# The second block's mixer projections in plain float32: one product on raw weights in place of three float32r products on split ones

## The chip, the cores and the metric

The kernel runs on one core of one Trainium2 chip. Such a core has TensorE (PE in the profile; its weight loads are listed apart as PEld), VectorE (DVE), ScalarE (ACT), GpSimd (POOL) and SyncE (SP), which here only issues DMA transfers. Each engine works through its own instructions in order, and semaphores order the engines among each other. The metric is the device time of one execution, in microseconds (us), lower being better.

## The reference

A residual stream of 256 tokens with 1024 channels goes through two models one after the other, each with two layers. The change touches the second model only, and in it one part of each layer, the mixer:

```python
hn = _modulate(_rms_norm(h, norm_g[l, 1]), sh2, sc2)
z = hn @ w_in[l]                       # 1024 -> 2564 columns
o_a = _differential_attention(qa, ka, va, ...)   # slices of z, normalised per head
o_b = _conformer_conv(z[..., CONV0:GMLP0], ...)  # gate, causal convolution of width 31, norm, swish
o_c = _chunked_spatial_gating(z[..., GMLP0:FOX_Q0], ...)
o_d = _forgetting_attention(qd, kd, vd, log_f)
mixed = jnp.concatenate([o_a, o_b, o_c, o_d], axis=-1)
h = h + g2[:, None, :] * (mixed @ w_out[l])      # 1024 -> 1024
```

Before and after the mixer stands a gated feed-forward part (`ffn1`, `ffn2`) with its own norm and modulation. All is float32.

## The kernel before

Activations lie feature-major: 128 channels on the partitions, 256 tokens in the free dimension, so that 1024 channels are eight "k tiles" of 256 columns. Every large product is built from steps of one k tile by 128 output columns, which accumulate in a PSUM bank.

**Three float32r products for one float32 product.** The kernel multiplies in the type float32r and splits both operands into a high and a low part to keep float32 accuracy. For a weight part of 128 x 1024 numbers, `split_to` (L223) has ACT cast the raw weights `raw` to `wh`, and then DVE or POOL subtract to get `wl`; `prog["pool"]` says that every so-many-th subtraction goes to POOL (1: all of them, 3: every third). Activations are split by `hilo` (L202: a cast on ACT, a subtraction on DVE). `mm3` (L284) then issues three matmuls into the same bank: high by high, low activation by high weight, high activation by low weight. An `Act` holds an activation's two parts; a `Shifted` holds the unnormalised activation with two more columns for the shift, so that the first chunk of a projection can run before the norm is known.

**The weight stream.** All large weights lie in one array in the order of use and are loaded in parts of up to 512 KB (`load_to`, L214), each by one DMA of the SP queue, into five buffers `raw`. A load is issued five parts ahead, a part is split three ahead, and the two halves have four buffers each. A load into a buffer waits until the last reader of its former content is done; the SP queue issues in order, so that what stands behind such a load waits with it.

**The order of the work.** The program is recorded in the order of the Python code. The projections go chunk by chunk (`chunk`, L268), and at each weight part `fill()` (L241) lets the background generators take a step: the norms of queries and keys, the convolution, the attentions, the spatial gate. Thus the products are interleaved on PE with the small matmuls of the attentions, and on DVE the 62 steps of the convolution with the norms.

**The mixer** (L1124 to L1382, twice). It loads two small tables `v2` and `ws` (in the profile `v` and `ws`) by the SP queue, and starts with instructions on them (`lp`, `ls`). Then: the first chunk M of 512 columns with the unnormalised activation (bank `m`); beside it the norm (`nrm`, `nu`, `rs`) and the normalised activation `h` (`xn`, `hh`, `hl`). The bank `m` goes through Tanh into the convolution `cv`. Four chunks of 256 columns give queries and keys (`qk`), each followed by its norm: square, matmul `qn`, a reciprocal root in three steps on DVE (`qu`, `qu`, `qr`), and the multiplication into `qk` or `fqk`. The scores `ds` of the first attention stand on PE right behind the fourth chunk. Chunks `gv` (260 columns), `gu` (256) and `mv` (512, weights as moving operand) follow, with the scores `ds`, `fs`, the convolution's norm `cc` and the transposes `tr` between them. The output projection N (`mo`) takes up the four branches (`mix`) two k tiles at a time. Per layer that is 21 weight parts of M and 8 of N. In the last quarter of the feed-forward part ahead of the mixer, `ffn` sets `prog["pool"] = 1` (L1108), which holds until the last part of N.

The names in the rows: `fd` is the bank of the feed-forward part's second product, `x` the residual stream, `xh`/`xl` its `Shifted` form, `f` the bank of the feed-forward part's first product, `sq` and `ssum` the sums of squares for the norm, `lfr` the forget gates of the second attention.

Of the kernel before, what the change touches and what calls it, by code (L numbers as in the profile page):

```python
# [24 lines left out]
RETH = 8  # L25
SUB_COLS = 1024
POOL_EVERY = 3
MLA_SCALE = (64 + 32) ** -0.5
# [94 lines left out]
def tile_model(ctx: ExitStack, tc: tile.TileContext, xT: bass.AP, pos: bass.AP, cvec: bass.AP, wst: bass.AP,  # L123
# [81 lines left out]

# [1 line left out]
    subs = _subs()  # L207
# [33 lines left out]
    def fill():  # L241
        """One step of each background part that is due."""
        prog["fill"] += 1
        for g in list(bgs):
            if prog["fill"] >= due[g]:
                step(g)

    def step(g):
        """A part yields the number of fills until its next step."""
        try:  # L250
            due[g] = prog["fill"] + next(g)
        except StopIteration:
            bgs.remove(g)
# [14 lines left out]
    def chunk(key, l, k0, kk, c0, cc):  # L268
# [6 lines left out]
        while s < len(subs) and subs[s][0] == j:  # L275
            split_to(s + 3)
            _, k, n, _, _ = subs[s]
            wh, wl = split.pop(s)
            for i in range(n):
                yield k0 + k + i, wh[:, i * cc:(i + 1) * cc], wl[:, i * cc:(i + 1) * cc]  # L280
            fill()
            s += 1
# [19 lines left out]
    def gemm_last(c, a, banks, klast, done):  # L302
        """The last part of a product, bank by bank, each followed by what takes it up."""
        parts = list(chunk(*c))
        for j in range(c[5] // 256):
            for k, wh, wl in parts:
                for e in range(2):
                    m = 2 * j + e
                    mm3(banks[j], banks[j].t[:, e * 256:e * 256 + 256], wh[:, m * P:(m + 1) * P],
                        wl[:, m * P:(m + 1) * P], a.h(k), a.l(k), k == klast)  # L310
# [11 lines left out]
    def gemm_shift(c, xa, banks, after):  # L322
        """The product with an unnormalised activation; the shift's products follow in two more columns."""
        for k, wh, wl in chunk(*c):
            if k == 2:
                after()
            for m, b in enumerate(banks):
# [3 lines left out]
                b.mm(b.t[:, :258], wb, xa.h(k), stop=k == 7)  # L331

    def pair_outs(banks):
        return {m: (banks[m // 2], m % 2) for m in range(2 * len(banks))}

# [1 line left out]
    nc.scalar.preload_act_table_set("silu_and_others")  # L337
# [43 lines left out]
    class Act:  # L381
        """A feature-major activation of n tiles as high and low float32r parts."""

# [7 lines left out]
        def l(self, k, n=1):  # L391
            return self.lo[k // 4][:, (k % 4) * 256:(k % 4 + n) * 256]

    gfa = const([P, 8], "gfa")
# [112 lines left out]

# [1 line left out]
    cond = []  # L509
# [503 lines left out]

    # =================== block 2 ===================
    rsx = rs_t
# [3 lines left out]
    def normalised(dst, l, i, first=False):  # L1019
        """rmsnorm(x) * g * (1 + scale) + shift in two parts, and the factor of the unnormalised product."""  # L1020
        if first:
# [10 lines left out]
        for j in range(4):  # L1032
            t_ = t2("xn")
            mul(v3(t_, 2), v3(xk(2 * j, 2), 2), bc(r, 2))
            for e in range(2):
                k = 2 * j + e
                nc.vector.tensor_scalar(out=t_[:, e * 256:(e + 1) * 256], in0=t_[:, e * 256:(e + 1) * 256],  # L1037
                                        scalar1=acol[:, k:k + 1],
                                        scalar2=mods[l][:, 24 * i + k:24 * i + k + 1], op0=ALU.mult, op1=ALU.add)
            hilo(t_, dst.h(2 * j, 2), dst.l(2 * j, 2))  # L1040
        if first:
# [9 lines left out]
    def following(l, i):  # L1051
        l, i = (l, i + 1) if i < 2 else (l + 1, 0)
        if l == L:
            return None
        return Shifted(l, i, lambda k: scl[l][:, 8 * i + k:8 * i + k + 1])

# [10 lines left out]

    def shift_bias(bank):
        b = small("bias", 1)
        nc.vector.tensor_reduce(out=b, in_=bank.t[:, 256:258], axis=AX.X, op=ALU.add)  # L1070
        return b

    def ffn(l, f, i, xa, first=False):
# [50 lines left out]
    def mixer(l, xa):  # L1124
# [29 lines left out]
        mix = Act(8, "mix")  # L1154

# [18 lines left out]
        def conv():  # L1174
# [26 lines left out]
            mul(v3(cv, 2), v3(bn_.t, 2), bc(r_, 2))  # L1201
            o_ = t2("co")
            for i in range(2):
                ins = act(o_[:, i * 256:(i + 1) * 256], cv[:, i * 256:(i + 1) * 256], AF.Silu,
                          scale=vc(f"cng{l}", i), bias=vc(f"cnb{l}", i))
            base_table(ins)
            hilo(o_, mix.h(4, 2), mix.l(4, 2))

        for i in range(2):
            ba, bg_ = b4[2 * i], b4[2 * i + 1]  # L1210
            ca, cg = shift_bias(ba), shift_bias(bg_)
            nc.vector.tensor_scalar_mul(cg, cg, 0.5)
# [10 lines left out]
        def diff(i):  # L1223
# [38 lines left out]
            rsqrt_eps(b.t[:, 0:256], r_, u_)  # L1262
            stt(r_, o_, dog, r_, ALU.mult, ALU.mult)
            hilo(r_, mix.h(6 + i), mix.l(6 + i))

        def fox(i):
# [32 lines left out]
            pv(b_o, lambda e, kb: vt[:, kb * 512 + 256 + (2 * i + e) * 64:kb * 512 + 320 + (2 * i + e) * 64], pts)  # L1299
            hilo(b_o.t[:, 0:256], mix.h(2 + i), mix.l(2 + i))  # L1300

# [3 lines left out]
        for n, (name, dst, blk, g) in enumerate((("qa", qk, "blk32", gq_), ("ka", qk, "blk32", vc(f"dqk{l}", 1)),  # L1305
                                                 ("fq", fqk_, "blk64", gf_), ("fk", fqk_, "blk64", vc(f"fqk{l}", 1)))):
            b = Bank("qk", True)
            gemm([("M", l, 0, 8, 512 + 256 * n, 256)], h.h, h.l, pair_outs([b]), 7)
# [3 lines left out]
        gemm_tok([("M", l, 0, 8, 1536, 260)], h.h, h.l, [(b, 0) for b in bg], 7)  # L1312
        vn = u4("vn", 512)
# [15 lines left out]
        def spatial():  # L1329
# [24 lines left out]
            mul(so, so, ut)  # L1354
            hilo(so, mix.h(0, 2), mix.l(0, 2))

        bu = Bank("gu", True)
        gemm([("M", l, 0, 8, 1796, 256)], h.h, h.l, pair_outs([bu]), 7)
        ins = act(ut, bu.t, AF.Gelu_apprx_tanh)
# [4 lines left out]
        bv = [Bank("mv", True) for _ in range(2)]  # L1364
        gemm_tok([("M", l, 4 * i, 4, 2052, 512) for i in range(2)], h.h, h.l, [(b, 0) for b in bv], 7)
        for t in range(2):
# [168 lines left out]
```

## Time and profile before

| | |
|---|---|
| Median of three runs | 2057.26 us (2048.43 to 2058.85) |
| Profiled execution: span from first to last instruction | 2054.9 us; what lies around the span is not shown, the median of the runs is 2.4 us longer |
| First mixer, from the first `m` product to the last `mo` product | 1162.06 to 1309.25 us: 147.2 us |
| Second mixer | 1706.69 to 1854.10 us: 147.4 us |
| PE busy / weight loads busy | 96% / 92% of the span |
| DVE, ACT, POOL busy | 72%, 51%, 35% |
| HBM traffic | 402.96 MB read, 197 GB/s over the span |

A matmul's busy time in the profile is from its start to its modelled end; matmuls overlap, so the pace of a stream is read from start to start in the timeline and not from the busy time of one. A float32 matmul of the program is recorded as two matmuls, one behind the other. The granted clock of PE (PEclk) is shown as a share of 2.4 GHz: 1.00 is that level, 0.50 is the other level of 1.2 GHz, and what lies between is a mean over a stretch.

### The profile page before, as it was taken

Reading aid. Unit: us, or ns where it says so; the run is one execution under the profiler, and the core shown is the slowest. Engines: PE = TensorE matmul, PEld = TensorE weight load, DVE = VectorE, ACT = ScalarE, POOL = GpSimd, SP = SyncE. Lnnn points to the kernel's source line nnn. Section 1 sums busy time; section 2 is a strip of 40 time slices with the busy share of each in tenths; the row PEclk is TensorE's granted clock in tenths of the full one; section 3 lists DMA queues with packets and bytes.
Section 4 is the critical chain, followed back from the end, with each engine's and each line's share of the span. In section 5 each row is a group of like instructions: output and inputs, shape, how many; then the busy total and the mean of one; then the engine's idle time right before and its main releaser. Section 6 shows DMA issues by size and latency. Waiting matters only on the chain. (4 is left out here: it accounts for less than half of the span.)

```text
span 2054.9 us, 38413 instructions
## 1 busy us (share of the span) xinstructions
PE 1966.4 (96%) x15570; PEld 1894.0 (92%) x15570; DVE 1480.6 (72%) x2076; ACT 1045.8 (51%) x1584; POOL 717.9 (35%) x339
## 2 busy tenths in 40 slices
PE   8999999999999999999999978998999998789999
PEld 7989999999989999999999966898999998679999
DVE  6778778696667778699877598888574446968443
ACT  5656555445556545345444446644454444455442
POOL 3232242323331343334223653422332246443222
PEclk9999999999999999999999989999999999899999
DMA  7545556885445656886667522388546554324553
GB/s 248 169 165 207 209 175 244 306 317 206 144 144 190 227 188 227 309 295 216 242 260 252 183 93 93 124 289 302 183 151 215 179 178 134 108 93 165 184 175 125
DMA packets 114946, 406.52 MB, mean 198 GB/s; under 512 B 12880, under 2 KB 14672, under 8 KB 114768
## 3 DMA queue, kind: packets, MB, share of 16 engines
q1 hardware_dynamic: 114768, 404.06, 56.6%
q8 instruction: 122, 2.00, 0.4%
q14 instruction: 56, 0.46, 0.1%
HBM read 402.96 MB, written 1.05 MB: 197 GB/s over the span
## 5 line engine op out<-in xcount | busy, mean ns | idle before, releaser
L233 POOL TENSOR_TENSOR wl<-raw,wh 128x1024 fp32r<-128x1024 f32 (+2 forms) x253 | 635.0, 2514 | 1257.7 <-ACT wh L231 1182.8
L231 ACT CAST wh<-raw 128x1024 fp32r<-128x1024 f32 (+1 forms) x627 | 641.4, 1030 | 614.7 <-PE fd L172 113.4
L233 DVE TENSOR_TENSOR wl<-raw,wh 128x1024 fp32r<-128x1024 f32 (+1 forms) x374 | 497.3, 1335 | 248.6 <-ACT wh L231 246.1
L172 PE MATMUL f<-hh,wl 128*128 128x256 f32 x1280 | 363.9, 285 | 4.9 <-POOL wl L233 4.0
L172 PE MATMUL f<-hl,wh 128*128 128x256 f32 x1280 | 364.2, 285 | 3.2 <-DVE hl L194 2.9
L172 PE MATMUL f<-hh,wh 128*128 128x256 f32 x1280 | 363.1, 284 | 4.3 <-ACT hh L203 3.1
L185 DVE SCALAR_TENSOR_TENSOR ada<-ada,cond 128x1024 f32<-128x1024 f32 x144 | 227.8, 1585 | 94.9 <-DMA ada<-ada_dram 94.6
L172 PEld LDWEIGHTS f<-hh,wl 128*128 128x128 f32 x1280 | 246.8, 193 | 6.4 <-POOL wl L233 4.6
L172 PEld LDWEIGHTS f<-hl,wh 128*128 128x128 f32 x1280 | 246.9, 193 | 4.8 <-DVE hl L194 4.8
L172 PEld LDWEIGHTS f<-hh,wh 128*128 128x128 f32 x1280 | 246.6, 193 | 5.1 <-ACT hh L203 3.7
L172 PE MATMUL fd<-hidh,wl 128*128 128x256 f32 x704 | 200.4, 285 | 4.0 <-DVE wl L233 3.5
L172 PE MATMUL fd<-hidh,wh 128*128 128x256 f32 x704 | 200.0, 284 | 0.6 <-DVE x L185 0.6
L172 PE MATMUL fd<-hidl,wh 128*128 128x256 f32 x704 | 199.9, 284 | 0.0
L172 PE MATMUL pr<-hh,wh 128*128 128x256 f32 x672 | 194.8, 290 | 0.0
L172 PE MATMUL pr<-hh,wl 128*128 128x256 f32 x672 | 190.1, 283 | 0.0
L172 PE MATMUL pr<-hl,wh 128*128 128x256 f32 x672 | 190.0, 283 | 0.0
L172 PE MATMUL dn<-hidh,wl 128*128 128x256 f32 x512 | 146.2, 285 | 3.6 <-DVE wl L233 3.6
L172 PE MATMUL u<-hh,wl 128*128 128x256 f32 x512 | 145.9, 285 | 2.6 <-DVE wl L233 2.6
L172 PE MATMUL u<-hh,wh 128*128 128x256 f32 x512 | 145.9, 285 | 0.0
L172 PE MATMUL dn<-hidh,wh 128*128 128x256 f32 x512 | 145.6, 284 | 0.0
L172 PE MATMUL dn<-hidl,wh 128*128 128x256 f32 x512 | 145.5, 284 | 0.0
L172 PE MATMUL u<-hl,wh 128*128 128x256 f32 x512 | 145.5, 284 | 0.0
(474 smaller groups left out, 4786.1 us busy)
## 6 DMA issues: line engine op xcount, KB each, us to landing
raw<-wst_dram SPq DMA_DIRECT2D x599, 512.0 KB, 4.0
ada<-ada_dram SPq DMA_DIRECT2D x144, 512.0 KB, 5.0
raw<-wst_dram SPq DMA_DIRECT2D x22, 256.0 KB, 2.8
raw<-wst_dram SPq DMA_DIRECT2D x4, 390.0 KB, 3.0
R<-ret_dram SPq DMA_DIRECT2D x2, 512.0 KB, 7.7
out_dram<-x SPq DMA_DIRECT2D x8, 128.0 KB, 3.3
C<-cst_dram SPq DMA_DIRECT2D x1, 896.0 KB, 7.7
v<-vec_dram SPq DMA_DIRECT2D x2, 448.0 KB, 5.7
```

The costliest lines, as they stand in the source:

```text
L172: nc.tensor.matmul(out, lhsT=lhsT, rhs=rhs, start=grp not in self.open, stop=stop, skip_group_check=True)
L185: nc.vector.scalar_tensor_tensor(out=out, in0=in0, scalar=s, in1=in1, op0=op0, op1=op1, **kw)
L231: nc.scalar.copy(wh[:, :n * cc], src)
L233: ins = eng.tensor_tensor(out=wl[:, :n * cc], in0=src, in1=wh[:, :n * cc].bitcast(F32), op=ALU.subtract)
```

## The change

The chunks of M and N are no longer split. `split_to` hands the raw part on as it was loaded, and the products take raw float32 weights and one float32 activation: a class `Plain` (one tile set in place of two) for `h` and `mix`, a class `ShiftedPlain` for the mixer's unnormalised activation with one more column in place of two. Each `mm3` of three float32r matmuls becomes one float32 matmul. With the halves go the casts and subtractions of these weights (29 parts per layer) and the second halves of `xa`, `h` and `mix`; the four results that fed a `hilo` are written straight into `mix`. The line that set `prog["pool"] = 1` ahead of the mixer goes, so the last weight parts of that feed-forward part are shared between DVE and POOL as the earlier ones are. (Removed comment lines are left out here.)

```diff
+NATIVE = ("M", "N")
...
-            _, _, n, cc, _ = subs[i]
+            j, _, n, cc, _ = subs[i]
+            if plan[j][0] in NATIVE:
+                split[i] = (raws.pop(i), None)
+                prog["split"] += 1
+                continue
...
+    def gemm_native(chunks, a, outs, klast):
+        for c in chunks:
+            for k, w, _ in chunk(*c):
+                for m in range(c[5] // P):
+                    bank, half = outs[m]
+                    bank.mm(bank.t[:, half * 256:half * 256 + 256], w[:, m * P:(m + 1) * P], a.f(k), stop=k == klast)
+    def gemm_tok_native(chunks, a, outs, klast):
...
+                    bank.mm(bank.t[:, c0:c0 + c[5]], a.f(k)[:, t * P:(t + 1) * P], w, stop=k == klast)
+    def gemm_shift_native(c, xa, banks, after):
...
+                b.mm(b.t[:, :257], w[:, m * P:(m + 1) * P], xa.f(k), stop=k == 7)
...
-            hilo(t_, dst.h(2 * j, 2), dst.l(2 * j, 2))
+            if not plain:
+                hilo(t_, dst.h(2 * j, 2), dst.l(2 * j, 2))
...
-            if m == 3:
-                prog["pool"] = 1 if i == 0 else 2
+            if m == 3 and i == 2:
+                prog["pool"] = 2
...
-        h, r = Act(8, "h"), rsx
+        h, r = Plain(8, "h"), rsx
...
-        gemm_shift(("M", l, 0, 8, 0, 512), xa, b4, lambda: next(normalised(h, l, 1)))
+        gemm_shift_native(("M", l, 0, 8, 0, 512), xa, b4, lambda: next(normalised(h, l, 1)))
...
-            stt(r_, o_, dog, r_, ALU.mult, ALU.mult)
-            hilo(r_, mix.h(6 + i), mix.l(6 + i))
+            stt(mix.f(6 + i), o_, dog, r_, ALU.mult, ALU.mult)
...
-                gemm([("N", l, 2 * i, 2, 0, 1024)], mix.h, mix.l, pair_outs(b4), 7)
+                gemm_native([("N", l, 2 * i, 2, 0, 1024)], mix, pair_outs(b4), 7)
```

**PE, between the second and third chunk of queries and keys in the first layer's mixer.** The rows before (`hh`, `hl` are the activation's halves, `wh`, `wl` the weight's):

```order
L172 MATMUL qk_13780<-hh_13580,wh_13713 128x256
L172 MATMUL qk_13780<-hl_13582,wh_13713 128x256
L172 MATMUL qk_13780<-hh_13580,wl_13714 128x256
L172 MATMUL qk_13851<-hh_13579,wh_13783 128x256
L172 MATMUL qk_13851<-hl_13581,wh_13783 128x256
L172 MATMUL qk_13851<-hh_13579,wl_13784 128x256
```

And the rows now, from the first chunk's end to the third chunk:

```order
L173 MATMUL qk_13667<-h_13559,raw_13511 128x256 x8
L173 MATMUL qk_13698<-h_13558,raw_13564 128x256 x8
L173 MATMUL qn_13713<-qsq_13696,C 128x512
L173 MATMUL qk_13698<-h_13559,raw_13574 128x256 x8
L173 MATMUL qk_13739<-h_13558,raw_13610 128x256 x8
L173 MATMUL qn_13754<-qsq_13737,C 128x512
```

Three matmuls of a product became one that reads the loaded buffer itself; the small matmuls stand at the same places between the chunks, here and in the rest of the mixer.

**POOL, from the last quarter of the first layer's first feed-forward part on.** Before, behind the third sum of squares (`ssum` x2), the subtractions of all the following weights, those of M and N among them:

```order
L374 TENSOR_TENSOR ssum<-ssum,sq_13367 128x256 x2
L233 TENSOR_TENSOR wl_13439<-raw_13317,wh_13438 128x1024
L233 TENSOR_TENSOR wl_13469<-raw_13347,wh_13468 128x512
L233 TENSOR_TENSOR wl_13499<-raw_13376,wh_13498 128x1024
L233 TENSOR_TENSOR wl_13529<-raw_13406,wh_13528 128x1024
```

Now, from the same sum to the end of the mixer and the next feed-forward part:

```order
L405 TENSOR_TENSOR ssum<-ssum,sq_13358 128x256 x2
L238 TENSOR_TENSOR wl_14413<-raw_14337,wh_14412 128x1024
L402 TENSOR_TENSOR ssum<-sq_14389 128x256
L405 TENSOR_TENSOR ssum<-ssum,sq_14402 128x256 x2
L405 TENSOR_TENSOR ssum<-ssum,sq_14422 128x256 x2
L238 TENSOR_TENSOR wl_14559<-raw_14377,wh_14558 128x1024
```

POOL has nothing to do during the mixer; its next subtraction belongs to the feed-forward part behind it.

**DVE, at the end of the first layer's first feed-forward part.** Before (`x<-fd` is the update of the residual stream, `lp` the first instruction on the table `v`):

```order
L185 SCALAR_TENSOR_TENSOR x<-fd_13196,hg_164,x 128x256 x2
L185 SCALAR_TENSOR_TENSOR xl_12813<-x,scl_162,xh_12810 128x256 x2
L1130 MEMSET yv_13554 128x576
L188 TENSOR_TENSOR lp_13562<-v_2050_13552 128x32 x2
L1138 TENSOR_REDUCE ls_13563<-lp_13562 128x1 x2
L185 SCALAR_TENSOR_TENSOR x<-fd_13375,hg_164,x 128x256 x2
L188 TENSOR_TENSOR ws_13553<-ws_13553,C 128x128 x3
```

Now:

```order
L238 TENSOR_TENSOR wl_13428<-raw_13308,wh_13427 128x1024
L238 TENSOR_TENSOR wl_13458<-raw_13338,wh_13457 128x512
L186 SCALAR_TENSOR_TENSOR x<-fd_13364,hg_164,x 128x256 x2
L1193 MEMSET yv_13533 128x576
L189 TENSOR_TENSOR lp_13541<-v_2044_13531 128x32 x2
L1201 TENSOR_REDUCE ls_13542<-lp_13541 128x1 x2
L189 TENSOR_TENSOR ws_13532<-ws_13532,C 128x128 x4
```

The last update of the stream stood behind the two instructions on the table and now stands ahead of them; among the last weight subtractions ahead of it two are now on DVE.

## Rows read from the trace of the kernel before

**Rows 1.** The page's head and part 1: engine, busy us (share), instructions.

```profile
span 2054.9 us, 38413 instructions
PE 1966.4 (96%) x15570; PEld 1894.0 (92%) x15570; DVE 1480.6 (72%) x2076; ACT 1045.8 (51%) x1584; POOL 717.9 (35%) x339
```

**Rows 2.** Stretches of both mixers: length, busy us (instructions) by engine, PEclk, DMA.

```profile
1162.06:1309.25 147.19, 122.05 (x833) 108.23 (x831) 126.44 (x246) 77.70 (x156) 73.82 (x30) 0.90 0.32 109
1706.69:1854.10 147.41, 120.82 (x833) 106.62 (x832) 125.08 (x245) 77.70 (x156) 74.06 (x30) 0.90 0.32 108
```

**Rows 3.** Waits of PE in the first mixer: us in total, times, longest.

```profile
PE ds L172 <- DVE qk L185: 8.9, 1, 8.9
PE cc L172 <- DVE cv L185: 4.7, 1, 4.7
PE fs L172 <- DVE lfr L1273: 3.5, 1, 3.5
PE nrm L172 <- ACT sq L378: 2.9, 1, 2.9
PE qk L172 <- ACT hh L203: 2.3, 2, 1.9
```

**Rows 4.** Stretches of 5 us around the wait of `ds`, columns as in Rows 2.

```profile
1215.00:1220.00 5.00, 0.00 (x0) 0.00 (x0) 5.00 (x10) 0.01 (x1) 0.77 (x1) 0.74 0.46 156
1220.00:1225.00 5.00, 4.00 (x21) 3.35 (x22) 5.00 (x12) 0.58 (x1) 0.00 (x0) 0.50 0.00 0
```

**Rows 5.** Timeline of PE, float32r products: start us, length us, instruction.

```profile
1199.25 0.28 PE L172 MATMUL qk<-hl,wh 128*128 128x256 f32 x1
...
1199.61 0.28 PE L172 MATMUL qk<-hl,wh 128*128 128x256 f32 x1
...
1242.70 0.39 PE L172 MATMUL mv<-wl,hh 128*128 128x512 f32 x1
...
1243.39 0.39 PE L172 MATMUL mv<-wl,hh 128*128 128x512 f32 x1
```

**Rows 6.** Timeline of PE, float32 products of 256 and 512 columns.

```profile
91.35 0.60 PE L172 MATMUL sc<-KE,Q 128*128 128x256 f32 x2
91.79 0.59 PE L172 MATMUL sc<-KO,Q 128*128 128x256 f32 x2
92.22 0.22 PE L172 MATMUL sc<-mkb,identb 128*128 128x128 bf16 x1
...
1194.69 1.02 PE L172 MATMUL qn<-qsq,C 128*128 128x512 f32 x2
...
1195.66 0.28 PE L172 MATMUL qk<-hl,wh 128*128 128x256 f32 x1
```

**Rows 7.** DVE in the first mixer, one group of lines: count, busy us, mean ns.

```profile
L185 DVE SCALAR_TENSOR_TENSOR cv<-yv,cw,cv 128x256 f32<-128x256 f32 x60 | 36.9, 660 | 0.0
```

**Rows 8.** Timeline of POOL and DVE in the first mixer.

```profile
1191.79 20.71 POOL L233 TENSOR_TENSOR wl<-raw,wh 128x1024 fp32r<-128x1024 f32 x7 [5.46 <-ACT wh L231]
...
1199.07 2.90 DVE L185 SCALAR_TENSOR_TENSOR qu<-qu,qr 128x512 f32<-128x512 f32 x1
...
1224.70 0.68 DVE L185 SCALAR_TENSOR_TENSOR qu<-qu,qr 128x512 f32<-128x512 f32 x1
1225.30 0.47 DVE L185 SCALAR_TENSOR_TENSOR cv<-yv,cw,cv 128x256 f32<-128x256 f32 x1
1225.70 0.68 DVE L185 SCALAR_TENSOR_TENSOR qr<-qu,qr 128x512 f32<-128x512 f32 x1
```

**Rows 9.** Timeline of SP and DVE at the start of the first mixer.

```profile
1159.02 0.42 SPq L1127 DMA_DIRECT2D v<-vec_dram  x1
...
1164.43 2.28 DVE L188 TENSOR_TENSOR lp<-v 128x32 f32<-128x32 f32 x2 [12.60 <-DMA v<-vec_dram]
...
1166.86 0.87 DVE L185 SCALAR_TENSOR_TENSOR x<-fd,hg,x 128x256 f32<-128x256 f32 x2
```

More of the change, by code (lines that the diff above doesn't have):

```diff
@@ L279, in chunk @@
             for i in range(n):
-                yield k0 + k + i, wh[:, i * cc:(i + 1) * cc], wl[:, i * cc:(i + 1) * cc]
+                yield k0 + k + i, wh[:, i * cc:(i + 1) * cc], wl[:, i * cc:(i + 1) * cc] if wl is not None else None
             fill()
@@ L308, in gemm_last @@
                     m = 2 * j + e
-                    mm3(banks[j], banks[j].t[:, e * 256:e * 256 + 256], wh[:, m * P:(m + 1) * P],
-                        wl[:, m * P:(m + 1) * P], a.h(k), a.l(k), k == klast)
-            done(j)
+                    out, cols = banks[j].t[:, e * 256:e * 256 + 256], slice(m * P, (m + 1) * P)
+                    if wl is None:
+                        banks[j].mm(out, wh[:, cols], a.f(k), stop=k == klast)
+                    else:
+                        mm3(banks[j], out, wh[:, cols], wl[:, cols], a.h(k), a.l(k), k == klast)
+            done(j)
+    def gemm_native(chunks, a, outs, klast):
[5 more added lines that the diff above has]
+    def gemm_tok_native(chunks, a, outs, klast):
+        for c in chunks:
+            for k, w, _ in chunk(*c):
+                for t in range(2):
+                    bank, c0 = outs[t]
+                    bank.mm(bank.t[:, c0:c0 + c[5]], a.f(k)[:, t * P:(t + 1) * P], w, stop=k == klast)
     def gemm_tok(chunks, ah, al, outs, klast):
@@ L331, in gemm_shift @@
                 b.mm(b.t[:, :258], wb, xa.h(k), stop=k == 7)
+    def gemm_shift_native(c, xa, banks, after):
+        for k, w, _ in chunk(*c):
+            if k == 2:
+                after()
+            for m, b in enumerate(banks):
+                b.mm(b.t[:, :257], w[:, m * P:(m + 1) * P], xa.f(k), stop=k == 7)
     def pair_outs(banks):
@@ L392, in l, with __init__, f, parts @@
             return self.lo[k // 4][:, (k % 4) * 256:(k % 4 + n) * 256]
+    class Plain:
+        def __init__(self, n, s):
+            self.t = [u4(s) for _ in range((n + 3) // 4)]
+        def f(self, k, n=1):
+            return self.t[k // 4][:, (k % 4) * 256:(k % 4 + n) * 256]
+    class ShiftedPlain:
+        def __init__(self, l, i, acol):
+            self.t = [u4("xf") for _ in range(3)]
+            self.acol = acol
+            for t in range(3):
+                n = min(3, 8 - 3 * t)
+                v = self.t[t][:, :n * 257].rearrange("p (k c) -> p k c", c=257)
+                nc.scalar.copy(v[:, :, 256], mods[l][:, 24 * i + 3 * t:24 * i + 3 * t + n])
+        def f(self, k, n=257):
+            return self.t[k // 3][:, (k % 3) * 257:(k % 3) * 257 + n]
+        def parts(self, j):
+            for k in (2 * j, 2 * j + 1):
+                act(self.f(k, 256), xk(k), AF.Identity, scale=self.acol(k))
     gfa = const([P, 8], "gfa")
@@ L1034, in normalised @@
             mul(v3(t_, 2), v3(xk(2 * j, 2), 2), bc(r, 2))
+            plain = isinstance(dst, Plain)
             for e in range(2):
                 k = 2 * j + e
-                nc.vector.tensor_scalar(out=t_[:, e * 256:(e + 1) * 256], in0=t_[:, e * 256:(e + 1) * 256],
-                                        scalar1=acol[:, k:k + 1],
+                nc.vector.tensor_scalar(out=dst.f(k) if plain else t_[:, e * 256:(e + 1) * 256],
+                                        in0=t_[:, e * 256:(e + 1) * 256], scalar1=acol[:, k:k + 1],
                                         scalar2=mods[l][:, 24 * i + k:24 * i + k + 1], op0=ALU.mult, op1=ALU.add)
-            hilo(t_, dst.h(2 * j, 2), dst.l(2 * j, 2))
+            if not plain:
+                hilo(t_, dst.h(2 * j, 2), dst.l(2 * j, 2))
         if first:
@@ L1054, in following @@
             return None
-        return Shifted(l, i, lambda k: scl[l][:, 8 * i + k:8 * i + k + 1])
+        return (ShiftedPlain if i == 1 else Shifted)(l, i, lambda k: scl[l][:, 8 * i + k:8 * i + k + 1])
     def gated_update(j, bank, l, i, nxt, part=None):
@@ L1066, in gated_update, with shift_bias @@
         nxt.parts(j)
-    def shift_bias(bank):
+    def shift_bias(bank, native=False):
         b = small("bias", 1)
-        nc.vector.tensor_reduce(out=b, in_=bank.t[:, 256:258], axis=AX.X, op=ALU.add)
+        if native:
+            nc.vector.tensor_copy(b, bank.t[:, 256:257])
+        else:
+            nc.vector.tensor_reduce(out=b, in_=bank.t[:, 256:258], axis=AX.X, op=ALU.add)
         return b
@@ L1299, in fox @@
             pv(b_o, lambda e, kb: vt[:, kb * 512 + 256 + (2 * i + e) * 64:kb * 512 + 320 + (2 * i + e) * 64], pts)
-            hilo(b_o.t[:, 0:256], mix.h(2 + i), mix.l(2 + i))
+            nc.scalar.copy(mix.f(2 + i), b_o.t[:, 0:256])
         gd = [launch(diff(i)) for i in range(2)]
@@ L1307, in mixer @@
             b = Bank("qk", True)
-            gemm([("M", l, 0, 8, 512 + 256 * n, 256)], h.h, h.l, pair_outs([b]), 7)
+            gemm_native([("M", l, 0, 8, 512 + 256 * n, 256)], h, pair_outs([b]), 7)
             launch(qknorm(b.t, dst[:, n % 2 * 512:n % 2 * 512 + 512], blk, g, name), 0)
         bg = [Bank("gv", True) for _ in range(2)]
-        gemm_tok([("M", l, 0, 8, 1536, 260)], h.h, h.l, [(b, 0) for b in bg], 7)
+        gemm_tok_native([("M", l, 0, 8, 1536, 260)], h, [(b, 0) for b in bg], 7)
         vn = u4("vn", 512)
@@ L1353, in spatial @@
                     bc(gms[:, i * P:(i + 1) * P], 2))
-            mul(so, so, ut)
-            hilo(so, mix.h(0, 2), mix.l(0, 2))
+            mul(mix.f(0, 2), so, ut)
         bu = Bank("gu", True)
-        gemm([("M", l, 0, 8, 1796, 256)], h.h, h.l, pair_outs([bu]), 7)
+        gemm_native([("M", l, 0, 8, 1796, 256)], h, pair_outs([bu]), 7)
         ins = act(ut, bu.t, AF.Gelu_apprx_tanh)
@@ L1364, in mixer @@
         bv = [Bank("mv", True) for _ in range(2)]
-        gemm_tok([("M", l, 4 * i, 4, 2052, 512) for i in range(2)], h.h, h.l, [(b, 0) for b in bv], 7)
+        gemm_tok_native([("M", l, 4 * i, 4, 2052, 512) for i in range(2)], h, [(b, 0) for b in bv], 7)
         for t in range(2):
```

8 lines of the change are left out of this document (3 added, 5 removed).

## The prediction

> **What bounds the kernel now.** The page's first part comes first: TensorE is busy for 96% of the span, its weight loads for 92%, VectorE for 72% [rows 1]. Averaged over all stages this is a kernel bound by PE. The change sits in two stretches only, so the second view is the table of stretches for them: each mixer lasts 147 us, and there PE is busy for 122.05 and 120.82 us only, at a mean granted clock of 0.90, while DVE is busy for 126 us and POOL for 74 [rows 2]. In the mixer PE is not the bound. The list of waits says who is: PE waited 8.9 us for the normalised queries and keys, 4.7 for the convolution, 3.5 for the forget gates, all of them on DVE, 2.9 for the sums of squares and 2.3 for the activation's high half [rows 3]. After such a wait PE comes back at the lower clock level: in the 5 us behind the longest idle stretch the granted clock was 0.50 [rows 4], which is 1.2 GHz.
>
> Why DVE is late shows in the timeline of POOL beside DVE. From 1191.79 POOL subtracts without a break for 20.7 us; in that time one step of the norm on DVE takes 2.90 us, and the same step at 1224.70, with POOL idle, 0.68 [rows 8]. The 60 listed convolution steps take 0.66 us in the mean against 0.47 for one beside an idle POOL [rows 7, 8], 11 us lost on this group alone.
>
> **Added on PE.** A float32r product of three matmuls with 256 columns goes from start to start in 0.36 us (1199.25 to 1199.61), one with 512 columns in 0.69 (1242.70 to 1243.39) [rows 5]. Float32 products with weights that change are in the trace too: from 91.35 to 92.22 stand four recorded matmuls, which are two products of 256 columns, so 0.435 us each [rows 6]. With 512 columns one product lasts from 1194.69 to 0.12 us ahead of 1195.66, 0.85 us [rows 6]. Per mixer there are 32 products in the first chunk, 64 for queries and keys, 16 in `gv`, 16 in `gu` and 64 in N, 192 of 256 to 260 columns: 192 x 0.075 = 14.4 us. The 16 of `mv` add 16 x 0.16 = 2.6. Together 17.0 us per mixer, 34 us in both, all on PE, and on the path wherever PE does not wait. The two products of rows 6 alone took 0.44 (91.35 to 91.79) and 0.43, which give 18 and 16 us as ends.
>
> The Trainium skill (FP8 and Floating Point Precision, TensorE Precision Notes) counts four passes through the array for true FP32. One pass per float32r matmul and the row's 0.12 us for each would give 0.48 us per product and 46 us for 384 products in place of 29. The two recorded matmuls at 0.217 us show less, so I take the rows.
>
> **What goes, and what that gives back.** POOL's subtractions in the mixer go, and with them what slows DVE; 29 casts per layer on ACT, the halves `hl` and `mixl` on DVE. What this can give back to PE is its waiting: 147.19 - 122.05 = 25.1 us in the first mixer, 147.41 - 120.82 = 26.6 in the second [rows 2], mean 25.9. The clock adds to it: 0.10 x 147 = 14.7 us per mixer, of which some falls on idle time anyway (0.26 x 5 = 1.3 us in the first of the two stretches of rows 4); I take 12, with 7 and 14.7 as ends. A wait also ends a dense stream with a matmul's drain, 0.28 in place of 0.12 us [rows 5]; some ten waits make 1.6 us. At most about 39.5 us per mixer come back.
>
> Does DVE then come in time? I follow it from T, the first product of the mixer, with DVE at the pace beside an idle POOL: a step of 512 columns 0.60 us, one of 256 columns 0.40 (1224.70, 1225.30, 1225.70) [rows 8].
> - The first chunk (32 x 0.435) and the norm's three products take PE until T+15.2. Queries and keys (64 x 0.435 = 27.8) and three `qn` (2.6) bring it to `ds` at T+45.6.
> - A new wait stands at the start. The sixth weight part of M goes into the buffer of the first, which is free only when PE has used it, at T+3.5. The transfers of `v` and `ws` are queued behind it on SP, and `lp` waits for `v` on DVE with the whole norm behind it. Issue to use of `v` took 1164.43 - 1159.02 = 5.4 us [rows 9]; with 0.5 us for the issue ahead of it `lp` starts at T+9.4. The table's instructions (about 1.8), three steps of the norm (1.2) and the first of `xn` and `h` (1.5) give the first k tile of `h` at T+13.9 and the last at T+17; PE asks for them at T+15.2 and from T+18.7 on. The margin is 1.3 us, so this wait costs nothing if the transfer takes no longer than before, and else what it is late. Its counterpart goes: the last update of `x` waited behind `lp` until 1166.86 though PE was done with `fd` at T = 1162.06 [rows 2, 9]; in the new order it stands ahead, so that the 2.9 us wait of the norm goes.
> - The convolution starts at about T+20. DVE has 23 of its steps (9.2), the query norm (4 x 0.60 + 3 x 0.40 = 3.6), ten steps (4.0), the key norm (3.6): `qk` is complete at T+40.4, and PE needs it at T+45.6. The 8.9 us wait goes, with 5 us to spare.
> - 62 convolution steps and four norms end by about T+57, with the softmax maxima between them; PE asks for `cc` at about T+72. The 4.7 us wait goes.
> - Behind that I count on small rests, where an attention's transposed weights or its output are copied by ACT and PE has one product to fill in: 2.5 us.
>
> **Costed at nothing.** In the last quarter of the feed-forward part DVE takes some four subtractions from POOL; it is idle for 12.60 us there [rows 9], and PE has three matmuls per product to hide them (a subtraction has twice the columns of a 0.60 us step [rows 8], so without that cover 4 x 1.2 = 5 us, and more beside POOL). Weight buffers are now held until PE has used them; a part lasts 8 x 0.435 = 3.5 us, a load has four parts, 14 us, and needs about 5.4 [rows 9]. If loads lost that cover, each of 29 parts could cost up to 2 us.
>
> **Sum.** Per mixer 39.5 - 17.0 - 2.5 = 20.0 us, 40 us in both; span 2054.9 - 40 = 2015, and with the 2.4 us by which the median lies above the profiled span, 2017 us. With all the ends against it (7 for the clock, 18 added, 8 of rests) it is 34.5 - 26 = 8.5 per mixer, 2040; with all for it (14.7, 16, none) 42.2 - 16 = 26.2, 2005.
>
> **Rivals.**
> - PE is the bound after all (slower). The rests of PE are tied to chains through ACT and PSUM that do not shorten, so that the longer products come on top: 2057 + 34 = 2091. For it speaks 96% in rows 1; against it that the three longest waits end with DVE and that DVE runs at a fraction of its pace just then. It decides from the point where less than 17 of the 39.5 us come back, for instance if `qk` comes later than T+46 + 9. The Trainium skill (Perfetto Trace Analysis, Identifying the Most-Contended Engine) takes the engine with the highest occupancy, for TensorE by its weight loads' share; by the 92% for the whole kernel that engine is TensorE, and more time on it must lengthen the run. By rows 2 the rule, taken stretch by stretch, names DVE.
> - DVE stays late for part of it: the new wait for `v` comes late, or `fs` and `cc` wait still. Two thirds back: 2 x (26.3 - 17.0) = 19, 2039. Half back: 2 x 2.7 = 5, 2052, which can't be told from no change.
> - The upper clock level isn't held in a long run of float32 matmuls. Rows 6 show four in a row at the full pace, no longer run. Twice the time for 192 x 0.435 + 16 x 0.85 = 97 us of products in each mixer is 194 us more, less the 40: some 2210.
>
> **How the numbers follow.** The forecast's case (2005 to 2030) gets 0.66, two thirds back 0.15 (2030 to 2045), half back or an equal trade 0.07, PE as the bound 0.09, the clock 0.03. The range of 2003 to 2045 holds the first two, 0.81. A measurement of this kernel can tell about 0.5%, 10 us, from no change: faster than 2047 are the first two cases and a part of the third, 0.82; within 10 us on both sides 0.06; slower 0.12.
>
> **What would show it.** In the profile after: recorded float32 matmuls of `qk` and `mo` at 0.217 us from start to start; both mixers at about 127 us with PEclk near 1.00; POOL almost idle in them; the convolution steps at 0.47 us in the mean; no wait of `ds` for `qk` nor of `cc` for `cv`; `lp` at T+9. The prediction is wrong if PE's idle time in the mixers stays above 10 us, if the products go slower than 0.45 us, or if the time moves outside the mixers.

## The result, and the profile after

Four runs of the changed kernel took 2004.91 us in the median (2002.21 to 2017.73), four of the kernel before, beside them, 2055.06 us (2048.43 to 2058.85). The ratio is 0.9774 with a 95% interval of 0.9748 to 0.9799: faster by 2.3%. The forecast was 2017 us, in a range of 2003 to 2045.

The page's first part of the kernel after, against [rows 1]:

```profile
span 2003.8 us, 37301 instructions
PE 1968.3 (98%) x15154; PEld 1872.6 (93%) x15154; DVE 1378.4 (69%) x2040; ACT 985.4 (49%) x1512; POOL 556.4 (28%) x275
```

PE's busy time hardly moved (1966.4 to 1968.3) while the span lost 51.1 us: what went is PE's idle time. The equal busy time is not equal work; the float32 products added some 33 us (below), and almost as much went with the lower clock and the broken streams of matmuls in the mixers. Where the idle time went, the stretches of both mixers show, with the columns of [rows 2], from the first `m` product to the first product of the next feed-forward part:

```profile
1160.74:1284.18 123.44, 123.44 (x624) 97.27 (x623) 80.39 (x233) 50.79 (x121) 3.19 (x2) 1.00 0.39 127
1678.81:1802.25 123.44, 123.44 (x624) 97.26 (x623) 80.05 (x231) 50.83 (x121) 3.19 (x2) 1.00 0.39 127
```

Both mixers last 123.44 us, 23.75 and 23.97 less than before: 47.7 of the 51.1 us. PE is busy in all of it at a granted clock of 1.00 (0.90 before), DVE went from 126 to 80 us, POOL from 74 to 3. The list of PE's waits for these stretches, [rows 3] before, has no entry at all. The other 3.4 us lie outside: 1.3 ahead of the first mixer, 2.8 between the two, -0.7 behind. They can't be told from scatter: in the traces of the kernel after and of the ten experiments below, whose work outside the mixers is the same but for a few subtractions, the first mixer starts between 1156.73 and 1164.65 us, and the stretch between the two is 393.7 to 398.2 us long (397.4 before).

Around the scores `ds`, where PE had its longest wait and the lower clock behind it [rows 4], two 5-us stretches of the kernel after:

```profile
1200.00:1205.00 5.00, 5.00 (x23) 4.03 (x22) 5.00 (x14) 1.32 (x2) 0.00 (x0) 1.00 0.42 152
1205.00:1210.00 5.00, 5.00 (x31) 3.88 (x31) 5.00 (x13) 1.19 (x4) 0.00 (x0) 1.00 0.30 107
```

DVE is still full here, PE is too, and the clock is at its upper level of 2.4 GHz.

The pace of the new products, from the timeline of PE (start, length, instruction, count of recorded matmuls; two of them are one product). They answer to [rows 5, 6]:

```profile
1187.13 7.07 PE L173 MATMUL qk<-h,raw 128*128 128x256 f32 x32
1194.03 1.02 PE L173 MATMUL qn<-qsq,C 128*128 128x512 f32 x2
...
1206.20 0.92 PE L173 MATMUL ds<-qk 32*128 32x128 f32 x8
...
1225.79 7.08 PE L173 MATMUL mv<-raw,h 128*128 128x512 f32 x16
1232.71 1.46 PE L173 MATMUL cc<-cv,C 128*128 128x256 f32 x6
```

From 1187.13 to 1194.03 are 6.90 us for 16 products of 256 columns, 0.431 us each; from 1225.79 to 1232.71 are 6.92 us for 8 products of 512 columns, 0.865 us each.

DVE's steps of the convolution, [rows 7] before, are at 0.475 us in place of 0.660:

```profile
L186 DVE SCALAR_TENSOR_TENSOR cv<-yv,cw,cv 128x256 f32<-128x256 f32 x60 | 25.0, 475 | 0.0
```

And the start of the first mixer in the timelines of SP and DVE, [rows 8, 9] before. `h` is the activation, `qk<-qk,V,qr` the last step of the key norm:

```profile
1164.78 0.43 SPq L1190 DMA_DIRECT2D v<-vec_dram  x1
```

```profile
1160.94 0.88 DVE L186 SCALAR_TENSOR_TENSOR x<-fd,hg,x 128x256 f32<-128x256 f32 x2 [8.81 <-PE fd L173]
1169.14 0.29 DVE L189 TENSOR_TENSOR lp<-v 128x32 f32<-128x32 f32 x2 [6.72 <-DMA v<-vec_dram]
1173.47 1.37 DVE L1096 TENSOR_SCALAR h<-xn,scl,mods 128x256 f32<-128x256 f32 x4
1175.97 1.38 DVE L1096 TENSOR_SCALAR h<-xn,scl,mods 128x256 f32<-128x256 f32 x4
1180.29 0.73 DVE L1245 TENSOR_SCALAR cv<-yv,cw,V 128x256 f32<-128x256 f32 x2
...
1199.97 0.74 DVE L186 SCALAR_TENSOR_TENSOR qk<-qk,V,qr 128x512 f32<-128x512 f32 x1
```

The update of `x` starts 0.2 us behind T = 1160.74, in the kernel before it started 4.8 us behind T [rows 2, 9]; the table `v` is issued at T+4.0, behind the load that waits for a buffer, and `lp` starts at T+8.4.

### The profile page after: what moved, and what is told of

It is laid out like the page before. It is cut to its first block, busy times and chain, and to the rows that moved or that the text cites. A ratio compares the mean times of both kernels' runs of the same rounds, so it can differ in the third digit from the quotient of the medians.

```text
span 2003.8 us, 37301 instructions
## 1 busy us (share of the span) xinstructions
PE 1968.3 (98%) x15154; PEld 1872.6 (93%) x15154; DVE 1378.4 (69%) x2040; ACT 985.4 (49%) x1512; POOL 556.4 (28%) x275
## 4 chain that ended last, share of the span: by engine, by line
PE 81%; DVE 8%; DMA 5%; issue 3%; ACT 1%; POOL 1%; SPq 0%; DVEq 0%; POOLq 0%; ACTq 0%
PE f L173 22%; PE pr L173 12%; PE fd L173 12%; PE dn L173 7%; PE br L173 3%; DMA ada<-ada_dram 3%; PE u L173 3%; PE qk L173 3%; DVE wl L238 2%; PE wo L173 2%; DMA raw<-wst_dram 2%; PE mo L173 1%; PE mv L173 1%; PE m L173 1%; DVE ada L186 1%
## 5 line engine op out<-in xcount | busy, mean ns | idle before, releaser
L236 ACT CAST wh<-raw 128x1024 fp32r<-128x1024 f32 (+1 forms) x569 | 582.2, 1031 | 581.7 <-PE fd L173 98.5
L238 POOL TENSOR_TENSOR wl<-raw,wh 128x1024 fp32r<-128x1024 f32 (+1 forms) x189 | 472.4, 2499 | 1365.3 <-ACT wh L236 1298.7
L238 DVE TENSOR_TENSOR wl<-raw,wh 128x1024 fp32r<-128x1024 f32 (+1 forms) x380 | 509.9, 1347 | 266.6 <-ACT wh L236 264.4
```

Of the source, the lines that this page charges most:

```text
L236: nc.scalar.copy(wh[:, :n * cc], src)
L238: ins = eng.tensor_tensor(out=wl[:, :n * cc], in0=src, in1=wh[:, :n * cc].bitcast(F32), op=ALU.subtract)
```

## The experiments

The theory behind the forecast, A: PE waited in the mixers because DVE was late, and DVE was late because POOL's subtractions held it up; off POOL, DVE comes in time, and PE's longer float32 products then fill what were waits. Rivals: the gain comes from the work that goes (casts on ACT, subtractions, second halves), or from the new order at the mixer's start. Each run was timed beside the kernel before; mixers are measured from the first `m` product to the first product of the next feed-forward part.

| kernel | median us | ratio to before, 95% | mixers us |
|---|---|---|---|
| before, subtractions of the mixer on DVE | 2021.86 | 0.9818 (0.9788 to 0.9848) | 130.2, 128.8 |
| after, with unused subtractions on POOL | 2036.80 | 0.9910 (0.9878 to 0.9942) | 140.8, 138.8 |
| after, with unused copies on POOL | 2012.21 | 0.9794 (0.9778 to 0.9811) | 126.1, 129.1 |
| after, with unused subtractions on DVE | 2017.05 | 0.9803 (0.9784 to 0.9822) | 128.4, 128.4 |
| after, with unused casts on ACT | 2007.18 | 0.9755 (0.9740 to 0.9769) | 124.2, 124.3 |
| after, with the removed `pool` line back | 2005.60 | 0.9760 (0.9744 to 0.9776) | 123.4, 123.4 |
| N in float32r | 1997.49 | 0.9724 (0.9709 to 0.9739) | 119.8, 119.7 |
| N and `mv` in float32r | 2004.36 | 0.9746 (0.9728 to 0.9763) | 120.7, 120.8 |
| after, beside the next | 2004.20 | 0.9760 (0.9746 to 0.9774) | 123.4, 123.4 |
| N in float32r, again | 1998.35 | 0.9732 (0.9719 to 0.9746) | 119.7, 119.7 |

**The kernel before with its subtractions on DVE.** One line, float32r stays (`len(subs)`, the number of all weight parts, leaves POOL none of the mixer's):

```diff
-                prog["pool"] = 1 if i == 0 else 2
+                prog["pool"] = len(subs) if i == 0 else 2
```

> The kernel before with one edit: around the mixer no weight subtraction goes to POOL, all of them go to DVE; the three float32r products stay. Theory A (the gain came from POOL's subtractions no longer slowing DVE, and from the PE waits that this slowness made): DVE's own work rises by 29 subtractions, some 33 us, to about 115 to 120 us per mixer, but each instruction runs at its full pace (convolution steps near 0.47 us); PE needs about 106 us of products, so the mixers fall from 147 to about 125 to 135 us, total 2015 to 2035. Theory B (the gain came from the removed work itself: casts, subtractions, second halves, three products of which one remains): no work goes here and DVE gets more, so the mixers stay at 147 us or grow, total 2055 to 2090.

Measured: 2021.86 us. The mixers, the largest waits of PE in the first, DVE's two largest groups there, and the group of the subtractions in the kernel before:

```profile
1162.77:1292.95 130.18, 118.33 (x832) 103.26 (x831) 113.28 (x272) 81.97 (x159) 3.56 (x3) 0.96 0.35 116
1688.86:1817.69 128.83, 115.61 (x832) 101.03 (x831) 113.27 (x271) 82.10 (x159) 3.56 (x3) 0.99 0.35 117
```

```profile
PE mv L172 <- DVE wl L233: 3.4, 3, 2.6
PE sg L172 <- DVE cw L1145: 2.1, 1, 2.1
PE mo L172 <- ACT dpT L589: 1.4, 1, 1.4
```

```profile
L233 DVE TENSOR_TENSOR wl<-raw,wh 128x1024 fp32r<-128x1024 f32 x25 | 30.4, 1218 | 4.6 <-ACT wh L231 4.6
L185 DVE SCALAR_TENSOR_TENSOR cv<-yv,cw,cv 128x256 f32<-128x256 f32 x60 | 25.9, 475 | 0.0
```

```profile
L233 DVE TENSOR_TENSOR wl<-raw,wh 128x1024 fp32r<-128x1024 f32 x2 | 2.9, 1467 | 0.0
```

The group of subtractions had 2 entries and 2.9 us on DVE in the first mixer before; it has 25 and 30.4 us now, three smaller ones take 2.6 more, and yet DVE is busy 13 us less (113.28 against 126.44 [rows 2]): POOL had cost it some 43 us there. The mixers lost 17.0 and 18.6 us without a float32 product. A holds, B (2055 and more) does not. The wait of `ds` for `qk`, 8.9 us before [rows 3], is gone; what is left is many waits, the longest of 2.6 us, most of them on a DVE that is full for most of the stretch.

The order at the mixer's start changes in this run too: the last update of `x` starts at 1163.64, ahead of `lp` at 1166.10, and the wait of the norm, 2.9 us before [rows 3], is gone. So some 3 of the 17.0 us can be the order's and not DVE's pace; no run has the order alone.

```profile
1163.64 0.87 DVE L185 SCALAR_TENSOR_TENSOR x<-fd,hg,x 128x256 f32<-128x256 f32 x2
1166.10 0.29 DVE L188 TENSOR_TENSOR lp<-v 128x32 f32<-128x32 f32 x2
```

**The kernel after with unused subtractions on POOL.** In `split_to`, for each part of M and N:

```diff
+                wl = wp.tile([P, SUB_COLS], F32R, tag="wl", bufs=4, name=nm("wl"))
+                src = split[i][0][:, :n * cc]
+                nc.gpsimd.tensor_tensor(out=wl[:, :n * cc], in0=src, in1=src, op=ALU.subtract)
```

> The kernel after with a subtraction on POOL for each of the 29 unsplit weight parts of a layer, whose result nothing uses; DVE, ACT and PE have the same instructions as in the kernel after. Theory A: POOL is busy again for some 60 to 75 us per mixer, DVE's steps are slow again (convolution steps near 0.66 us, DVE busy about 115 us), waits of PE for DVE return, and the mixers grow from 123.4 to 140 to 160 us, total 2040 to 2080. Theory B: POOL's work is off the path, the mixers stay within 3 us of 123.4, total 2000 to 2012.

Measured: 2036.80 us, 32 us of the gain of 50 lost again with not one more instruction on PE, DVE or ACT. Stretches of the mixers, and the two largest waits in the first:

```profile
1158.11:1298.91 140.80, 130.16 (x624) 101.34 (x623) 105.64 (x232) 50.71 (x121) 58.30 (x28) 0.95 0.34 111
1694.31:1833.06 138.75, 128.38 (x625) 99.73 (x623) 105.07 (x233) 50.92 (x122) 58.23 (x28) 0.96 0.34 113
```

```profile
PE ds L173 <- DVE qk L186: 6.3, 1, 6.3
PE fs L173 <- ACT dp L663: 2.3, 1, 2.3
```

DVE's same work takes 25 us longer (105.64 against 80.39), `ds` waits for `qk` again, and the clock falls to 0.95. A holds in kind; 2036.80 is under its 2040 to 2080, the second mixer 1.2 us under its 140, with POOL busy for 58 us and not the 60 to 75 expected, DVE for 106 and not 115. The new order at the mixer's start stays in this run (`x` at 1158.31, `lp` at 1166.52), so the 17.4 and 15.3 us by which the mixers are longer are POOL's alone.

**With copies on POOL in place of the subtractions.**

```diff
-                nc.gpsimd.tensor_tensor(out=wl[:, :n * cc], in0=src, in1=src, op=ALU.subtract)
+                nc.gpsimd.tensor_copy(wl[:, :n * cc], src)
```

> The kernel after with a copy on POOL (one operand read, one written) for each of the 29 unsplit weight parts of a layer, in place of the dummy subtraction (two operands read); the result is not used. Theory A (any elementwise work on POOL slows DVE while it runs): DVE's convolution steps at about 0.55 to 0.6 us as with the dummy subtraction, mixers 135 to 142 us, total 2025 to 2040. Theory B (only two-operand work on POOL does): steps at 0.47 us, mixers 123 to 125 us, total 2003 to 2010.

Measured: 2012.21 us, between both. The first mixer, and the convolution steps in it:

```profile
1158.51:1284.57 126.06, 124.20 (x624) 97.65 (x623) 90.74 (x233) 50.59 (x121) 31.73 (x26) 1.00 0.38 125
```

```profile
L186 DVE SCALAR_TENSOR_TENSOR cv<-yv,cw,cv 128x256 f32<-128x256 f32 x60 | 30.8, 568 | 0.0
```

The steps are as slow as A says (0.568 us), so copies disturb DVE too; the mixers are not as long as A says. POOL is busy for 31.73 and 29.98 us instead of 58.30 and 58.23, and DVE for 10 and 12 us longer than in the kernel after instead of 25. The loss goes roughly with the time that POOL works beside DVE: for each us that POOL has more to do than in the kernel after, DVE lost 0.36 and 0.43 us with the copies, 0.46 and 0.45 with the subtractions. Of the 10 and 12 us only 2.6 and 5.6 reach the mixers' length, of the 25 some 17.4 and 15.3.

**The kernel after with unused subtractions on DVE.** The three lines as on POOL, but for the engine:

```diff
-                nc.gpsimd.tensor_tensor(out=wl[:, :n * cc], in0=src, in1=src, op=ALU.subtract)
+                nc.vector.tensor_tensor(out=wl[:, :n * cc], in0=src, in1=src, op=ALU.subtract)
```

> The kernel after with a subtraction on DVE for each of the 29 unsplit weight parts of a layer, whose result nothing uses. Theory A (the kernel after is bound by PE in the mixers, with DVE full only from T+20 to T+50 and 5 us to spare before the scores): some 33 us more on DVE per mixer, about a third of it before the scores of the first attention, so that these wait some 5 us again and the convolution's norm little; mixers 125 to 133 us, total 2008 to 2025. Theory B (DVE's amount of work was the bound, not its pace): mixers near 123 + 33 = 156 us, total 2070. Theory C (DVE has slack everywhere): no change, 2005.

Measured: 2017.05 us. First mixer, and all waits of PE in it:

```profile
1162.43:1290.86 128.43, 124.78 (x625) 98.07 (x623) 105.09 (x257) 53.74 (x124) 3.20 (x2) 1.00 0.37 123
```

```profile
PE cc L173 <- DVE gr L186: 2.5, 1, 2.5
PE fs L173 <- ACT fp L663: 1.2, 1, 1.2
```

The same subtractions that cost 17.4 and 15.3 us per mixer on POOL cost 5.0 on DVE, at the same busy time of DVE, 105 us. A's size holds, B falls. Its place was wrong: `ds` did not wait, the late parts are the convolution's norm `cc` and the scores `fs`.

**The kernel after with unused casts on ACT.** In the same place:

```diff
+                wh = wp.tile([P, SUB_COLS], F32R, tag="wh", bufs=4, name=nm("wh"))
+                nc.scalar.copy(wh[:, :n * cc], split[i][0][:, :n * cc])
```

> The kernel after with a cast on ACT for each of the 29 unsplit weight parts of a layer, whose result nothing uses. Theory A: ACT goes from 51 to about 78 us of 123 per mixer and stays off the path, total within 5 us of the kernel after, 2000 to 2010. Theory B (the relief of ACT carried part of the gain: Tanh, Square, Exp came late behind casts): waits of PE on ACT return, 5 to 15 us per mixer, total 2015 to 2035.

Measured: 2007.18 us; mixers 124.2 and 124.3 us, 0.8 more than without, with ACT busy for 73 in place of 51 us. ACT's relief is worth under 1 us per mixer.

**The kernel after with the `pool` line back.**

```diff
-            if m == 3 and i == 2:
-                prog["pool"] = 2
+            if m == 3:
+                prog["pool"] = 1 if i == 0 else 2
```

> The kernel after with the line put back that gives all subtractions of the last quarter of the feed-forward part ahead of the mixer to POOL (three per layer move from DVE to POOL; the mixers themselves have none). Theory A (the line is worth nothing, the mixers' gain is all inside them): mixers at 123 to 125 us, total within 5 us of the kernel after, 2000 to 2010. Theory B (part of the gain, above all the end of the 2.9 us wait of the norm and the earlier last update of the residual stream, comes from these subtractions on DVE): POOL's slower subtractions hold up the last products of the feed-forward part or the update, 3 to 8 us per layer more, total 2012 to 2022.

Measured: 2005.60 us, mixers 123.44 and 123.44 us. The subtractions that moved from POOL to DVE in the feed-forward part cost and bring nothing, as the prediction had it.

**N in float32r.** Now that PE is dense in the mixers and DVE is at 80 of 123 us, the cheaper products should pay where DVE has room. `NATIVE = ("M",)`, the branches are split again by `hilo`, and the subtractions stay off POOL (the lines that split the branches are left out):

```diff
-NATIVE = ("M", "N")
+NATIVE = ("M",)
...
-            if m == 3 and i == 2:
-                prog["pool"] = 2
+            if m == 3:
+                prog["pool"] = len(subs) if i == 0 else 2
...
-                gemm_native([("N", l, 2 * i, 2, 0, 1024)], mix, pair_outs(b4), 7)
+                gemm([("N", l, 2 * i, 2, 0, 1024)], mix.h, mix.l, pair_outs(b4), 7)
```

> The kernel after with the output projection N back in three float32r products on split weights and split branches, all its subtractions (8 parts per layer) on DVE and none on POOL; M stays float32. Theory A (the mixers of the kernel after are bound by PE's dense float32 stream, DVE has slack behind T+50): 64 products give 0.07 us each, 4.6 us per mixer, mixers at 119 to 120 us, total 1993 to 1999. Theory B (N waits for the branches as soon as PE is faster, or for the cast and subtraction that now stand between a branch and N): the 4.6 us turn into waits of mo, mixers at 123 to 126 us, total 2003 to 2010.

Measured: 1997.49 us. The first mixer and its one wait:

```profile
1159.86:1279.61 119.75, 119.34 (x689) 96.64 (x688) 92.21 (x248) 60.29 (x135) 3.56 (x3) 1.00 0.41 137
```

```profile
PE mo L173 <- ACT dpT L647: 0.4, 1, 0.4
```

3.7 us per mixer, of 4.6 worked out; A.

**N and `mv` in float32r.** The same, and the chunk `mv`, with halves of `h` made ahead of `gu`:

```diff
-            if plan[j][0] in NATIVE:
+            if plan[j][0] in NATIVE and plan[j][4] < 2052:
...
+        hs = Act(8, "h")
+        for k in (0, 4):
+            hilo(h.f(k, 4), hs.h(k, 4), hs.l(k, 4))
...
```

> As the run with N in float32r, and the chunk mv (512 columns) too, with the halves of h made just ahead of the chunk gu. Theory A (PE bound, DVE with slack): 16 products give another 0.17 us each, 2.8 us per mixer, mixers at 116 to 118 us, total 1988 to 1995. Theory B (DVE has no room for the 5 us of weight subtractions and 2.5 us for the halves between T+45 and T+72): the convolution's end and the norm cc come late as in the run with the dummy subtractions on DVE, mixers 120 to 125 us, total 1997 to 2010.

Measured: 2004.36 us; all waits of PE in the first mixer:

```profile
PE mo L173 <- ACT dpT L647: 1.9, 1, 1.9
PE sg L173 <- DVE vn L192: 0.7, 1, 0.7
PE fs L173 <- DVE lfr L1336: 0.4, 1, 0.4
```

Of the 2.8 us of shorter products 1.7 show in PE's busy time (119.34 to 117.63), the waits rise from 0.4 to 3.0 us, and the mixers are 0.9 and 1.1 us longer than with N alone. B by its size, but by other waits than it named: `cc` is not among them, the longest is that of the last products for ACT's copies of an attention's transposed weights. The rest of the distance to 1997.49 (mixers of this trace 2.0 us longer in sum, span 11.2 us) lies outside the mixers: the first begins 4.8 us later than with N alone, and the stretch between the two is 4.5 us longer. Why is open; both are the highest of the eleven traces named above, by 1.9 and 0.5 us, and the profiled run was the longest of its five (2007.23 us).

**The better version beside the kernel after,** on one chip:

> The kernel after, unchanged, timed on the same chip and beside the same runs of the kernel before as the version with N in float32r. Theory A (that version is faster by its 4 us per mixer): 2003 to 2008, with the other at 1995 to 1999. Theory B (the difference came from the chip and the runs it was compared with): the two within 3 us of each other.

> The version with N in three float32r products and its subtractions on DVE, again, beside the kernel after. Theory A: 1995 to 1999, 0.3 to 0.5% below the kernel after, mixers at 120 us. Theory B: within 3 us of the kernel after.

Measured: 2004.20 (2002.69 to 2009.47) and 1998.35 us (1997.33 to 2003.49); the ratios 0.9760 and 0.9732 to the same runs of the kernel before, with intervals that just touch at 0.9746. The traces say the same as those above: 123.44 us per mixer against 119.74. With N in float32r the kernel beats both, by about 6 us the one of this change.

## Why the prediction was right, and what it mis-sized

The mechanism was right, and the time came 12 us under the forecast, 2 us above the range's lower end and where the prediction's case with all for it (2005) had put it. The four runs spread over 2002.21 to 2017.73, so that it fell inside the range is in part luck.

- *PE isn't the bound in the mixers, DVE is, and POOL makes it late.* Shown from both sides: POOL's subtractions taken out of the kernel before give 17.0 and 18.6 us per mixer (some 3 of them perhaps by the order at its start), put into the kernel after they cost 17.4 and 15.3.
- *Added on PE: 17.0 us per mixer.* By the rows after, a float32r product of 0.36 us [rows 5] became 0.431, 192 times, 13.7 us; one of 0.69 became 0.865, 16 times, 2.8 us. Measured 16.5. The other price weighed in the prediction, 0.48 us, did not come; the rows decided rightly. The 0.48 took the Trainium skill's four passes for true FP32 (FP8 and Floating Point Precision, TensorE Precision Notes) at a float32r matmul's 0.12 us each. Four times 256 periods of the granted 2.4 GHz are 0.427 us, by estimate, so the measured 0.431 speaks against that pace for a pass and not against the four.
- *Given back: at most 39.5 us, less 2.5 of rests.* Measured 23.9 + 16.5 = 40.4. This is the term that was mis-sized: there are no rests (0 in place of 2.5, 5.0 us in both mixers), and waits, clock and drains gave 0.9 more (1.7 in both). All 25.9 us of waits went, so the 0.9 lies with clock and drains: 14.5 in place of 13.6, not told apart. With the 0.5 on PE (1.0 in both) that makes 7.7 us of the 11.2 by which the span of 2003.8 lies under the forecast's 2015; the other 3.4 lie outside the mixers, within the scatter between traces.
- *The course from T,* predicted and measured: `lp` T+9.4, T+8.4 (the transfer took 4.4 us from issue to use, not 5.4); first `h` T+13.9, T+13.1 (one of the four that start at T+12.7), and the last complete at T+16.6, before PE asked; convolution T+20, T+19.6; `qk` complete T+40.4, T+40.0; `ds` T+45.6, T+45.5; `cc` T+72, T+72.0. The margin of 5 us ahead of `ds` was there, and it is what POOL's subtractions used up when they came back and `ds` waited 6.3 us.
- *Costed at nothing.* The shared subtractions: shown, by the `pool` line put back. The longer hold of the weight buffers: no product waits for a load in the mixers, where PE has no wait at all.
- *The rivals.* PE as the bound after all fell: it needed less than 17 us to come back, and 40.4 did. That DVE stays late for part fell with the empty list of waits. That the upper clock level isn't held fell: 123.44 us of products, nearly all float32, at 1.00. The rival of the experiments, the new order at the mixer's start, was not tried apart; the 2.9 us of the norm's wait are the only wait that the rows tie to it, and POOL's subtractions cost 17.4 and 15.3 us with the new order in place.

What the prediction did not see is that the float32 products were not what the larger part of the gain hung on. Of the 23.9 us per mixer, 17.8 come with one line that takes POOL out and leaves three products, and then the step from there to the kernel after pays 16.5 us on PE to get 22.6 back. Of these 12.5 are the waits that were left (130.18 - 118.33 and 128.83 - 115.61, mean), the rest clock and drains. They do not add up from single causes: the unused subtractions on DVE cost 5.0, the casts 0.8. A reading that no run here shows by itself: with float32r DVE is busy for 113 of 130 us and PE, with some 107 us of work (123.4 - 16.5), waits for it in many places; with float32 PE's longer work lies in that waiting time. How much the halves `hl` and `mixl`, which also went, carry of it was not tried apart.

## What to carry to other kernels

Read the bound for the stage that a change touches: over the span PE was at 96%, in the two mixers it waited a sixth of the time. Before replacing work on a full engine, look at which neighbour holds it up, since taking the neighbour's work away may be the larger part of the gain and one line long. And once a stage's bound has moved, ask again for each part of the change: with PE dense, the cheaper float32r products paid for N, and no longer when `mv` was added, where new waits took more than the products gave.

## What the runs showed of the hardware

POOL doesn't slow DVE, it stops it. The timeline of POOL and DVE in the run with unused subtractions on POOL, and the durations (shortest, median, longest, in ns) of these subtractions in its first mixer:

```profile
1185.64 7.20 DVE L186 SCALAR_TENSOR_TENSOR cv<-yv,cw,cv 128x256 f32<-128x256 f32 x18
1186.31 13.84 POOL L233 TENSOR_TENSOR wl<-raw 128x1024 fp32r<-128x1024 f32 x4 [3.24 <-DMA raw<-wst_dram]
1192.77 0.74 DVE L186 SCALAR_TENSOR_TENSOR qu<-qn,eps,qr 128x512 f32<-128x512 f32 x1
1193.43 1.45 DVE L186 SCALAR_TENSOR_TENSOR cv<-yv,cw,cv 128x256 f32<-128x256 f32 x1
1194.81 2.38 DVE L186 SCALAR_TENSOR_TENSOR qu<-qu,qr 128x512 f32<-128x512 f32 x1
```

```profile
L233 POOL TENSOR_TENSOR wl<-raw x26: 1054/1895/8292, 1157.0 to 1284.6; 128x1024 fp32r<-128x1024 f32 x23, 128x780 fp32r<-128x780 f32 x2, 128x520 fp32r<-128x520 f32 x1
```

While 18 steps of the convolution run back to back, 0.4 us apart, POOL's subtraction does not end: it is the one of 8.3 us, in place of 1.9. It comes through at a step on `qn`, which lies in PSUM, and from then on each of the next steps with both operands in SBUF lasts until POOL's instruction is done and 0.3 to 0.6 us more: 1.45, 2.38. So DVE loses the time of whole instructions of POOL, and here POOL lost that of a whole run of steps on DVE. The Trainium skill (SBUF — State Buffer, Who interferes with whom) says that DVE shares its second pair of SBUF ports with GpSimd, that a DVE instruction with two inputs in SBUF contends with a GpSimd instruction that reads SBUF, and that who issues first has the pair for its whole instruction while the other is blocked. The trace agrees, with 0.68 us for such a step beside an idle POOL [rows 8] and 2.38 here.

That POOL is held out for a whole run is seen once in each mixer, at the same place, in this run (8.29 and 8.39 us) and in the kernel before (7.07 and 7.05). It is not the rule: a later subtraction of the same run, and a copy of the run with copies, come in between two steps of the convolution.

```profile
1223.60 2.90 DVE L186 SCALAR_TENSOR_TENSOR cv<-yv,cw,cv 128x256 f32<-128x256 f32 x3
1223.81 2.03 POOL L233 TENSOR_TENSOR wl<-raw 128x1024 fp32r<-128x1024 f32 x1 [12.36 <-DMA raw<-wst_dram]
```

```profile
1183.50 2.04 DVE L186 SCALAR_TENSOR_TENSOR cv<-yv,cw,cv 128x256 f32<-128x256 f32 x3
1184.22 1.04 POOL L233 CAST wl<-raw 128x1024 fp32r<-128x1024 f32 x1 [2.11 <-DMA raw<-wst_dram]
```

Three steps take 2.90 and 2.04 us there, and 1.27 beside an idle POOL. Why the one subtraction waited and the others did not is open.

A stretch without waits repeats far better than the kernel: the six mixers of the three kernels with all products in float32 and nothing added to the engines (the kernel after, the same again, and the one with the `pool` line back) all took 123.44 us, while the parts around them differ by some us from trace to trace.
